# Preparing q and k of the next pair of heads during the second head of the pair before, in the attention of a two-layer decoder

## The chip, the core and the metric

The kernel runs on one core of a Trainium2 chip. A core has five engines that run side by side, each with its own queue that is worked off strictly in order: PE (TensorE, matrix multiplications and transposes), DVE (VectorE), ACT (ScalarE), POOL (GpSimd) and SP (SyncE, which here only issues transfers). PE's weight loads are shown as PEld; they overlap its multiplications. The metric is the time of one execution on the device in microseconds (us), lower is better.

## The reference

The program is a decoder of two layers over 512 tokens of 1024 features, in float32. Each layer is attention, a projection with a residual, and an MLP with a squared ReLU. Layer 0 mixes 8 heads of dilated attention (kind "a") with 8 heads of sliding-window attention that share two key heads (kind "b"); layer 1 has 16 heads of forgetting attention (kind "c"). A head has 64 features; q and k are normalised per head.

```python
def reference(x, ...):
    for layer in range(DEPTH):
        h = rms_norm(x, g_mix[layer])
        if layer % 2 == 0:
            x = x + even_mixer(h, ...)     # heads a and b
        else:
            x = x + odd_mixer(h, ...)      # heads c
        h = rms_norm(x, g_mlp[layer])
        x = x + squared_relu_mlp(h, w_up[layer], w_down[layer])
    return x

def forgetting_attention(q, k, v, log_f):          # one block of 128 queries
    s = jnp.einsum("bqhd,bshd->bhqs", qb, k) * scale
    s = s + jnp.transpose(cq, (0, 2, 1))[..., None] - c_k[:, :, None, :]
    s = jnp.where((key_pos[None, :] <= t[:, None])[None, None], s, -jnp.inf)
    p = jax.nn.softmax(s, axis=-1)
    return jnp.einsum("bhqs,bshd->bqhd", p, v)
```

## The kernel before

Float32 products are made of three products of a high and a low part, so that every weight tile is split first (`whi` on POOL or ACT, `wlo` on POOL or DVE) and every projection is three matmuls: `pj` in the input projections (lines 231 to 233) and `op` in the output projection (lines 164, 167, 168).

Heads are worked in pairs, because two heads of 64 features fill the 128 partitions. `get(p_)` prepares pair p_: `head_T` (line 263) transposes 128 columns of the normalised q, and for the kinds a and c of k, into a PSUM bank named `qkT`, four transposes each. `prep_q` turns it into the tile `Q` with, for each head, a copy on ACT (line 277) and a subtraction on DVE (line 278). `prep_k` makes a tile `K` for each head (ACT line 159, DVE line 160), then SP copies half of it to the other partitions with a transfer (line 290). For the kind b, K is made once before the first pair, and `get` prepares q alone afterwards.

Then come the two heads of the pair (`scores`, line 302). For each of four query blocks PE makes the scores `S` (lines 325, 326, for kind c a mask at 328), DVE adds a bias and takes the minimum (`P`, `negm`, line 339), ACT takes the exponential (line 342), DVE the reciprocal (line 345), and POOL or ACT scales the row. `values` (line 353) transposes P on PE (`PT`, line 362), splits it on ACT and DVE (lines 374, 375), and multiplies by V (`O`, line 382); ACT and DVE add the two halves into `yf` (lines 385, 386). The values of a head are made while the scores of the following head are, one step behind.

For the kind c each head's bias is a transfer of its own (line 311). The buffers that matter: `qkT`, `S`, `PT` and `O` all take one of four PSUM banks (tag `pB`); there are two Q tiles, three K tiles, and two bias tiles.

All of this is one generator, `attend`. `run` advances it against a second generator of dense work, mostly input projections of a later group, by counting steps. A scheduler then orders the instructions within each engine, starting from that program order and moving some of them past each other; it also picks the free bank. There are seven groups: a(0), b and a(1) in layer 0, c(0) to c(3) in layer 1; a group of kind a or c has two pairs and b has four.

Of the kernel before, what the change touches and what calls it, by code (L numbers as in the profile page):

```python
# [37 lines left out]
NORM = 'vgvg'  # L38
PSC = 'ggga'
GRAIN = 4  # L40
STARTPIN = 4
JPIN = 1
PEPIN = True
# [29 lines left out]
def trunk(ctx, tc, x, g_mix, g_mlp, w_in_even, a_q_gain, a_k_gain, b_q_gain, b_k_gain, b_sinks,  # L73
# [46 lines left out]

    cnt = {"hi": 0, "start": STARTPIN}

# [69 lines left out]
    def layer_attention(li, hT, w_in, w_out, stats=None):  # L192


        with ExitStack() as c2:
# [11 lines left out]
            def project(cols, use, pat=PAT_ATT, ahead=False):  # L207
# [6 lines left out]
                for k0 in range(0, DC, kw):  # L214
# [9 lines left out]
                    for m in range(NT if last else kw):  # L224
                        for k, t in ([(k0 + kk, m) for kk in range(kw)] if last else [(k0 + m, t) for t in range(NT)]):
# [8 lines left out]
                            pairs += 1  # L234
                            if pairs % GRAIN == 0:
                                yield GRAIN / 32 * n
                use(outs)
# [153 lines left out]
            def head_values(prev):  # L391
                if prev is None:
                    return
                pr, kind, V, vs, yf, j, n = prev
                yield from values(pr, kind, V, vs, yf, j)
                if j:
                    y = slot(f"y{li}_{n}")
                    ys[n] = y
                    split(y[:, 0], y[:, 1], yf, "act", YLO)

            last_head = [None]

            def attend(get, koff, V, vslot, kind, h0, np_, y0):

                for p_ in range(np_):
                    q, kk = get(p_)
                    yf = ap.tile([P, 512], F32, tag="yf", bufs=1, name="yf")
                    yield
                    for j in range(2):
                        h = h0 + 2 * p_ + j  # L410
                        pr = []
                        old = head_values(last_head[0])
                        for i, _ in enumerate(scores(q, kk[j], j, kind, h, pr)):
                            yield
                            if i >= LAGS["abc".index(kind)] and next(old, 0) is None:
                                yield
                        for _ in old:
                            yield
                        last_head[0] = (pr, kind, V(), vslot(2 * p_ + j), yf, j, y0 + p_)
# [89 lines left out]
            if li == 0:  # L509
# [7 lines left out]
                def att_a(g):  # L517
                    def get(p_):
                        qk = st["qk", g]
                        return prep_q(qk, p_ * P), prep_k(qk, 256 + p_ * P, gg[:, 0:1])  # L520
                    return attend(get, 256, lambda: st["v", g], lambda j: j, "a", 4 * g, 2, 2 * g)
# [7 lines left out]
                def att_b():  # L529
                    def get(p_):  # L530
                        if p_ == 0:
                            st["kb"] = prep_k(st["k", "b"], 0, gg[:, 1:2])
                        k = st["kb"][p_ // 2]
                        return prep_q(st["qk", "b"], p_ * P), [k, k]
                    return attend(get, 0, lambda: st["v", 3], lambda j: j // 4, "b", 0, 4, 4)

                tables, first, qk0 = make_tables(ap, dist, lt, lb), start(ap, hT), qk_a(0)
                next(tables)
                for i, n in enumerate((1, 1 + 8 // GRAIN, 1 + 8 // GRAIN, 1 + 8 // GRAIN)):
                    cnt["start"] = i < STARTPIN  # L540
                    next(first)
# [4 lines left out]
                cnt["start"] = False  # L546
                for _ in range(8 // GRAIN):
                    next(qk0)
# [8 lines left out]
            else:  # L557
# [12 lines left out]
                def att_c(g):  # L570
                    def get(p_):
                        qk = st["qk", g]
                        return prep_q(qk, p_ * P), prep_k(qk, 256 + p_ * P, gg[:, 2:3])
                    return attend(get, 256, lambda: st["v", g], lambda j: j, "c", 4 * g, 2, 2 * g)
# [166 lines left out]
    def mlp(li, accs, attention_end, last):  # L741
# [5 lines left out]
        with ExitStack() as c2:  # L747
# [468 lines left out]
            return hn, lambda: col_stats(token_sums(res["ssum2"]))  # L1216

    accs, end = layer_attention(0, [], w_in_even[0], w_out_even[0])
    hT, stats = mlp(0, accs, end, False)
    accs, end = layer_attention(1, hT, w_in_odd[0], w_out_odd[0], stats)  # L1220
    mlp(1, accs, end, True)

# [21 lines left out]
```

## Time and profile before

| what | value |
|---|---|
| runs of the kernel | 1172.76 us median of 3 (1170.35 to 1174.13) |
| the profiled execution, its own time | 1169.99 us |
| its span | 1168.2 us |
| instructions | 17496 |
| PE busy / weight loads busy | 98% / 84% of the span |
| DVE, ACT, POOL busy | 75%, 55%, 17% |
| attention of layer 0, attention of layer 1 (rough limits) | 46 to 222 us, 610 to 825 us |

The span runs from the first instruction to the last; the execution's own time is 1.8 us longer. Busy time is the time in which an engine works on at least one instruction. An engine's idle time is put down to what ended it.

### The profile page before, as it was taken

The page shows a single profiled execution, that of the slowest core. Times are in us where ns is not written, and L with a number is a line of the kernel's source. Part 1 is how long each engine was busy: PE and PEld are TensorE (multiplying, and loading weights), DVE is VectorE, ACT ScalarE, POOL GpSimd, SP SyncE. Part 2 cuts the span into 40 slices and gives each one's busy share as a digit, 9 for nine tenths or more (in the row PEclk, how much of TensorE's full clock was granted, in tenths as well). Part 3 has the DMA queues.
Part 4 walks back from the last instruction along what each step waited for, and adds up shares of the span by engine and source line. Part 5 has one row for each costly group of instructions (what it writes and reads, how often), then busy time and mean ns, then how long its engine had stood idle before and what let it go on. Part 6 is the DMA issues. An engine that isn't in the chain of part 4 may idle for free.

```text
span 1168.2 us, 17496 instructions
## 1 busy us (share of the span) xinstructions
PE 1146.4 (98%) x6256; PEld 981.4 (84%) x6256; DVE 879.8 (75%) x1870; ACT 646.6 (55%) x1349; POOL 203.0 (17%) x296
## 2 busy tenths in 40 slices
PE   8999989999999999999999999999999999999998
PEld 7987878887988988988887888888888888888887
DVE  7878999969947847855647877788858749669676
ACT  6556867655445545444335685656756455465452
POOL 1445434200000000000155445332100000000000
PEclk9999999999999999999999999999999999999999
DMA  7532024132332332333443323343430721623403
GB/s 257 160 91 73 19 73 145 58 123 73 101 117 91 91 108 91 96 121 108 148 127 109 103 89 110 100 124 112 163 106 3 232 91 51 202 73 108 148 34 109
DMA packets 100655, 126.57 MB, mean 108 GB/s; under 512 B 6184, under 2 KB 79944, under 8 KB 100568
## 3 DMA queue, kind: packets, MB, share of 16 engines
q1 hardware_dynamic: 99384, 121.23, 34.0%
q10 hardware_dynamic: 608, 2.13, 0.5%
q0 software_dynamic: 576, 2.10, 0.4%
q8 instruction: 49, 0.80, 0.3%
q14 instruction: 38, 0.31, 0.1%
HBM read 112.29 MB, written 6.32 MB: 102 GB/s over the span
## 4 chain that ended last, share of the span: by engine, by line
PE 82%; DVE 9%; DMA 3%; ACT 2%; POOL 1%; issue 1%; SPq 0%; ACTq 0%; POOLq 0%; DVEq 0%
PE up L164 10%; PE up L167 10%; PE up L168 10%; PE pj L231 4%; PE pj L233 4%; PE pj L232 4%; PE O L382 3%; PE PT L362 2%; PE Y L1023 2%; PE Y L1022 2%; PE Y L1020 2%; PE op L168 2%; PE op L164 2%; PE op L167 2%; PE S L325 2%; DVE wlo L155 1%
## 5 line engine op out<-in xcount | busy, mean ns | idle before, releaser
L164 PE MATMUL up<-xin,whi 128*128 128x512 f32 x512 | 200.5, 392 | 0.0
L168 PE MATMUL up<-xin,whi 128*128 128x512 f32 x512 | 199.3, 389 | 0.0
L167 PE MATMUL up<-xin,wlo 128*128 128x512 f32 x512 | 199.2, 389 | 0.0
L769 ACT CAST whi<-wraw 128x512 fp32r<-128x512 f32 x228 | 139.2, 619 | 105.5 <-PE up L168 47.3
L770 DVE TENSOR_TENSOR wlo<-wraw,whi 128x512 fp32r<-128x512 f32 x228 | 151.7, 686 | 53.7 <-ACT whi L769 53.5
L168 PEld LDWEIGHTS up<-xin,whi 128*128 128x128 f32 x512 | 96.1, 188 | 20.1
L164 PEld LDWEIGHTS up<-xin,whi 128*128 128x128 f32 x512 | 96.1, 188 | 19.9 <-issue 0.2
L167 PEld LDWEIGHTS up<-xin,wlo 128*128 128x128 f32 x512 | 96.2, 188 | 19.7 <-issue 0.2
L342 ACT ACTIVATE P<-P,negm 128x128 f32<-128x128 f32 (+5 forms) x128 | 69.6, 544 | 51.8 <-DVE negm L339 47.9
L231 PE MATMUL pj<-whi,hn 128*128 128x512 f32 (+2 forms) x256 | 88.7, 346 | 0.0
L951 ACT ACTIVATE u<-up 128x512 f32<-128x512 f32 x64 | 38.3, 598 | 90.9 <-PE up L168 90.9
L233 PE MATMUL pj<-whi,hn 128*128 128x512 f32 (+2 forms) x256 | 86.9, 339 | 0.0
L232 PE MATMUL pj<-wlo,hn 128*128 128x512 f32 (+2 forms) x256 | 86.8, 339 | 0.0
L152 POOL TENSOR_SCALAR whi<-wraw 128x512 fp32r<-128x512 f32 x88 | 61.1, 696 | 141.5 <-PE pj L233 121.3
L790 DVE TENSOR_TENSOR t<-u 128x256 f32<-128x256 f32 x56 | 23.2, 424 | 63.3 <-ACT u L1094 61.5
L155 POOL TENSOR_TENSOR wlo<-wraw,whi 128x512 fp32r<-128x512 f32 x48 | 64.4, 1345 | 20.8 <-ACT whi L150 18.1
L231 PE MATMUL pj<-whi,h 128*128 128x512 f32 (+1 forms) x192 | 65.6, 348 | 0.7 <-DVE v L160 0.7
L232 PE MATMUL pj<-wlo,h 128*128 128x512 f32 (+1 forms) x192 | 65.3, 341 | 0.2 <-DVE wlo L155 0.2
L233 PE MATMUL pj<-whi,h 128*128 128x512 f32 (+1 forms) x192 | 65.5, 343 | 0.0
L350 POOL TENSOR_SCALAR P<-P,rden 128x256 f32<-128x256 f32 (+2 forms) x96 | 47.7, 500 | 90.8 <-DVE rden L345 90.1
L155 DVE TENSOR_TENSOR wlo<-wraw,whi 128x512 fp32r<-128x512 f32 (+1 forms) x72 | 49.7, 697 | 17.5 <-POOL whi L152 9.8
L374 ACT CAST PT<-PT 128x256 fp32r<-128x256 f32 (+3 forms) x128 | 49.5, 405 | 19.3 <-PE PT L362 18.5
(229 smaller groups left out, 3051.7 us busy)
## 6 DMA issues: line engine op xcount, KB each, us to landing
wraw<-in_w_up SPq DMA_DIRECT2D x64, 512.0 KB, 4.0
wraw<-in_w_down SPq DMA_DIRECT2D x56, 512.0 KB, 4.2
wraw<-in_w_in_odd SPq DMA_DIRECT2D x36, 256.0 KB, 3.4
mraw<-in_w_down SPq DMA_DIRECT2D x16, 512.0 KB, 4.7
K<-K SPq DMA_DIRECT2D x26, 256.0 KB
wraw<-in_w_in_even SPq DMA_DIRECT2D x10, 512.0 KB, 4.0
wraw<-in_w_in_even SPq DMA_DIRECT2D x16, 256.0 KB, 4.5
xl<-xsp SPq DMA_DIRECT2D x8, 512.0 KB
```

The source lines that it names most:

```text
L152: nc.gpsimd.tensor_scalar(dst_h, src, 1.0, 1.0, op0=OP.mult, op1=OP.mult)
L155: in_order((nc.gpsimd if lo == "pool" else nc.vector).tensor_sub(dst_l, src, dst_h.bitcast(F32)))
L164: m = nc.tensor.matmul(o, wh, xh, start=start, stop=False, skip_group_check=more)
L167: nc.tensor.matmul(o, wl, xh, start=False, stop=False, skip_group_check=more)
L168: nc.tensor.matmul(o, wh, xl, start=False, stop=stop, skip_group_check=more)
L231: nc.tensor.matmul(o, xh, hi[:, :n], start=k == 0, stop=False)
L232: nc.tensor.matmul(o, xh, lo[:, :n], start=False, stop=False)
L233: nc.tensor.matmul(o, xl, hi[:, :n], start=False, stop=k == DC - 1)
L342: nc.scalar.activation(p[:, :ne], p[:, :ne], AF.Exp, scale=-1.0, bias=negm[:, i:i + 1], accum_out=den[:, i:i + 1])
L374: nc.scalar.copy(dst[:, 0], pt[:, :n])
L769: sca(nc.scalar.copy(dst_h, src))
L770: late.append(lambda: vec(nc.vector.tensor_sub(dst_l, src, dst_h.bitcast(F32))))
```

## The change

`attend` gets a list `pair`. When the second head of a pair (j = 1) has had its first query block of scores recorded (i = 0, the constant PRE), and there is a next pair in the group, `get(p_ + 1)` is called there and its result is kept; the next pair takes it from the list. Nothing else is changed: no instruction is added or removed. The first pair of each of the seven groups is prepared where it was; one pair is moved in each of the six groups of kind a and c (q and k), and three in b (q alone).

```diff
@@ -400,10 +401,12 @@
             last_head = [None]
 
+            pair = []
+
             def attend(get, koff, V, vslot, kind, h0, np_, y0):
 
                 for p_ in range(np_):
-                    q, kk = get(p_)
+                    q, kk = pair.pop(0) if pair else get(p_)
                     yf = ap.tile([P, 512], F32, tag="yf", bufs=1, name="yf")
                     yield
                     for j in range(2):
@@ -412,6 +415,8 @@
                         old = head_values(last_head[0])
                         for i, _ in enumerate(scores(q, kk[j], j, kind, h, pr)):
                             yield
+                            if j and i == PRE and p_ + 1 < np_:
+                                pair.append(get(p_ + 1))
                             if i >= LAGS["abc".index(kind)] and next(old, 0) is None:
                                 yield
```

How the instructions stand now. In the rows below, lines of the changed kernel are one higher than before in these functions (267 becomes 268, and so on).

PE in group c(1), before, from the last values of the first head of pair 0 to the first scores of pair 1. `pj` is the dense work, of which 24 rows stand between the transposes and the scores.

```order
L382 MATMUL O<-PT,v_6422 128x512 x2
L382 MATMUL O<-PT,v_6422 128x384 x2
L382 MATMUL O<-PT_6423,v_6422 128x256
L267 MATMUL qkT<-ident,qk 128x128
L382 MATMUL O<-PT_6423,v_6422 128x256 x3
L267 MATMUL qkT<-ident,qk 128x128 x7
L233 MATMUL pj_7563<-whi,hn 128x512
...
L232 MATMUL pj_7563<-wlo,hn 128x512
L325 MATMUL S<-K,Q 128x256
```

The same engine and group in the changed kernel: first the second head of pair 0, into which the transposes are put, then the place where pair 1 begins.

```order
L268 MATMUL qkT<-ident,qk 128x128 x8
L326 MATMUL S<-K,Q 128x256
L327 MATMUL S<-K,Q 128x256
L329 LDWEIGHTS identb
L329 MATMUL S<-maskb,identb 128x128
L363 MATMUL PT<-ident,P 128x128 x4
L234 MATMUL pj_7560<-whi,hn 128x512
L326 MATMUL S<-K,Q 128x384
...
L383 MATMUL O<-PT_6423,v_6422 128x256
L326 MATMUL S<-K,Q 128x256
L383 MATMUL O<-PT_6423,v_6422 128x256 x3
```

The transposes have moved up by about one head, the 24 dense matmuls that followed them are spread over that head and the next, and pair 1 begins among the values of the head before it. After the scores of 384 columns come 11 `pj` and then the next three transposes `PT`, which in the built program take the bank that q's `qkT` leaves.

DVE at the same place, before, where the four conversions of Q and K follow each other:

```order
L386 TENSOR_TENSOR yf<-O,yf 64x512
L278 TENSOR_TENSOR Q<-qkT,Q 64x512
L160 SCALAR_TENSOR_TENSOR K<-qkT,gg,K 64x512
L278 TENSOR_TENSOR Q<-qkT,Q 64x512
L160 SCALAR_TENSOR_TENSOR K<-qkT,gg,K 64x512
L155 TENSOR_TENSOR wlo<-wraw,whi 128x512
L339 ISA P,negm<-S,bias 128x128
```

And in the changed kernel:

```order
L387 TENSOR_TENSOR yf<-O,yf 64x512
L340 ISA P,negm<-S,bias 128x256
L340 ISA negm 128x1
L346 RECIPROCAL rden<-den 128x1
L156 TENSOR_TENSOR y_1_7543<-yf,y_1_7543 128x512
L279 TENSOR_TENSOR Q<-qkT,Q 64x512
L161 SCALAR_TENSOR_TENSOR K<-qkT,gg,K 64x512
L346 RECIPROCAL rden<-den 128x1
L279 TENSOR_TENSOR Q<-qkT,Q 64x512
L376 TENSOR_TENSOR PT<-PT 128x512
L161 SCALAR_TENSOR_TENSOR K<-qkT,gg,K 64x512
L340 ISA P,negm<-S,bias 128x384
```

The conversions now stand between the softmax steps of the second head, and one step of it (the 384 columns) stands behind the last of them.

SP in group c(0), before: the two transfers of K for pair 1 stand behind two weight loads and the second bias load.

```order
L183 DMA wraw<-in_w_in_odd 128x2x256 x2
L311 DMA bias<-csp 128x512
L183 DMA wraw<-in_w_in_odd 128x4x256
L311 DMA bias<-csp 128x512
L183 DMA wraw<-in_w_in_odd 128x4x256
L290 DMA K<-K 64x1024 x2
```

And in the changed kernel, where they have moved ahead of those three:

```order
L184 DMA wraw<-in_w_in_odd 128x2x256 x2
L312 DMA bias<-csp 128x512
L291 DMA K<-K 64x1024 x2
L184 DMA wraw<-in_w_in_odd 128x4x256
L312 DMA bias<-csp 128x512
L184 DMA wraw<-in_w_in_odd 128x4x256
```

## Rows read from the trace of the kernel before

**Rows 1.** The page: busy us, share of the span and instructions of each engine.
```profile
PE 1146.4 (98%) x6256; PEld 981.4 (84%) x6256; DVE 879.8 (75%) x1870; ACT 646.6 (55%) x1349; POOL 203.0 (17%) x296
```

**Rows 2.** Windows: stretch, its us, busy us by engine, PE's clock, DMA, GB/s.
```profile
46.00:107.00 61.00, 58.11 (x339) 49.70 (x338) 47.29 (x135) 32.97 (x84) 31.24 (x44) 1.00 0.33 96
107.00:180.00 73.00, 69.45 (x451) 60.26 (x450) 68.10 (x216) 54.88 (x160) 33.28 (x72) 1.00 0.16 46
180.00:222.00 42.00, 41.00 (x210) 33.18 (x209) 37.97 (x86) 25.77 (x60) 15.60 (x20) 1.00 0.41 126
610.00:700.00 90.00, 87.79 (x529) 74.03 (x528) 70.14 (x196) 56.82 (x139) 43.03 (x57) 1.00 0.36 103
700.00:825.00 125.00, 124.10 (x757) 106.71 (x756) 98.52 (x255) 74.02 (x175) 49.83 (x64) 1.00 0.38 112
```

**Rows 3.** PE's waits over the span: us in total, times, longest us.
```profile
PE S L325 <- DMA K<-K: 2.6, 3, 1.2
PE S L325 <- DVE Q L278: 1.8, 2, 1.5
PE S L325 <- DVE yf L386: 1.8, 2, 1.6
```

**Rows 4.** Timeline of PE: start us, us, instruction, [idle before <- what ended it].
```profile
151.84 0.39 PE L325 MATMUL S<-K,Q 128*128 128x256 f32 x1 [1.52 <-DVE Q L278]
...
161.52 0.39 PE L325 MATMUL S<-K,Q 128*128 128x256 f32 x1 [1.61 <-DVE yf L386]
...
649.66 0.36 PE L325 MATMUL S<-K,Q 128*128 128x256 f32 x1 [0.88 <-DMA K<-K]
...
795.56 0.36 PE L325 MATMUL S<-K,Q 128*128 128x256 f32 x1 [0.47 <-DMA K<-K]
```

**Rows 5.** Timeline of PE where pair 1 of a(0) is prepared.
```profile
71.34 1.03 PE L267 MATMUL qkT<-ident,qk 128*128 128x128 f32 x8
72.14 0.47 PE L231 MATMUL pj<-whi,h 128*128 128x512 f32 x1
72.45 0.40 PE L232 MATMUL pj<-wlo,h 128*128 128x512 f32 x1
...
77.47 0.28 PE L325 MATMUL S<-K,Q 128*128 128x256 f32 x1
```

**Rows 6.** Timeline of ACT there.
```profile
71.98 0.58 ACT L277 CAST Q<-qkT 64x512 fp32r<-64x512 f32 x1 [2.59 <-PE qkT L267]
...
73.31 0.58 ACT L277 CAST Q<-qkT 64x512 fp32r<-64x512 f32 x1 [0.17 <-DVE Q L278]
```

**Rows 7.** Timeline of DVE there.
```profile
72.59 0.68 DVE L278 TENSOR_TENSOR Q<-qkT,Q 64x512 fp32r<-64x512 f32 x1 [0.23 <-ACT Q L277]
73.31 0.74 DVE L160 SCALAR_TENSOR_TENSOR K<-qkT,gg,K 64x512 fp32r<-64x512 f32 x1
74.08 0.70 DVE L278 TENSOR_TENSOR Q<-qkT,Q 64x512 fp32r<-64x512 f32 x1
74.81 0.76 DVE L160 SCALAR_TENSOR_TENSOR K<-qkT,gg,K 64x512 fp32r<-64x512 f32 x1
```

**Rows 8.** The chain that ended last, at pair 1 of c(0): start us, us, what.
```profile
646.05 3.47 DMA K<-K
```

**Rows 9.** Windows: the stretch of group b with the long waits.
```profile
147.00:163.00 16.00, 12.77 (x97) 11.60 (x96) 15.78 (x45) 10.01 (x31) 8.26 (x13) 1.00 0.19 66
```

**Rows 10.** Timeline of DVE in that stretch.
```profile
147.85 1.52 DVE L308 SCALAR_TENSOR_TENSOR bias<-dist,lb 128x256 f32<-128x256 f16 x1
149.37 0.41 DVE L308 SCALAR_TENSOR_TENSOR bias<-dist,lb 128x256 f32<-128x256 f16 x1
...
157.67 3.00 DVE L260 TENSOR_TENSOR qk<-qk,rs 128x512 f32<-128x512 f32 x2
```

**Rows 11.** Timeline of PE in c(0): scores and transposes of one head.
```profile
657.28 0.36 PE L325 MATMUL S<-K,Q 128*128 128x256 f32 x1
...
657.67 0.61 PE L362 MATMUL PT<-ident,P 128*128 128x128 f32 x4
658.03 0.42 PE L325 MATMUL S<-K,Q 128*128 128x384 f32 x1
...
658.58 0.55 PE L362 MATMUL PT<-ident,P 128*128 128x128 f32 x3
```

More of the change, by code (lines that the diff above doesn't have):

```diff
@@ L40 @@
 GRAIN = 4
+PRE = 0
 STARTPIN = 4
```

## The prediction

> **What bounds the kernel now.** I read the page first: PE is busy for 1146.4 us of the span of 1168.2 [rows 1], so it stands still for 21.8 us in all, and no reordering can give back more than that. The change touches attention alone, so the second view is the windows of the attention stretches [rows 2]: they last 391 us, PE is busy in 380.45 of them (58.11 + 69.45 + 41.00 + 87.79 + 124.10), and 10.55 us are left. PE's clock column is 1.00 throughout. DVE is the second engine: 68.10 of 73 us in the stretch that holds group b, but only 98.52 of 125 in the last one. Third come PE's waits [rows 3]. Three of them are for the transfer of K (2.6 us), two for the subtraction of Q (1.8 us), two for `yf` (1.8 us). Fourth, the timeline tells which of these belong to a pair that the change moves [rows 4]: 1.52 us before the first scores of the last pair of b, 0.88 us at pair 1 of c(0), 0.47 us at pair 1 of c(3). That is 2.87 us at three of the nine moved places; at the other six PE does not wait at the pair's first scores. The rest of the waits for K and Q (the longest for K, 1.2 us, among them) belong to first pairs of a group, which stay, and the 1.61 us for `yf` stand inside a head.
>
> **What is moved.** Nothing is added, so the whole sum is waits that go and waits that come. A pair of kind a or c moves eight transposes, four conversions on ACT, four on DVE and two transfers on SP; a pair of b moves four transposes and two conversions on each engine. Why the old place costs so little is seen at pair 1 of a(0) [rows 5]: the transposes start at 71.34 and the first scores at 77.47, and the 6.1 us between are filled with 23 dense matmuls, one every 0.228 us (72.45 to 77.47 is 22 of them). The preparation is long, but PE is not idle in it. In the new order this dense work is still there and stands elsewhere, so hiding the preparation better is worth nothing where it is already hidden.
>
> **What is gained.** At c(0) about 12 us of PE work now lie between the transposes and pair 1, counted from the new order at the rates of [rows 5, 11], and a K transfer took 3.47 us [rows 8]: the 0.88 us go. At c(3) it is about 10 us; the 0.47 us go. The 1.52 us in b are another matter. DVE is busy 15.78 of 16 us there, and PE 12.77 [rows 9]. What makes Q late is that DVE is behind: one bias operation takes 1.52 us where the next of the same shape takes 0.41, and two scalings of `qk` for a later group take 3.00 us together [rows 10]. None of this is moved. Q's two subtractions (0.7 us each) leave the critical place, but the same DVE work must be done in the same stretch, and an engine with 0.22 us to spare in 16 gives back nothing but what is taken out of it. PE will meet DVE's lag at another scores or transposes. The bounds for this stretch are 0 (the lag only moves) and 3.13 us (both long waits of [rows 4] go, 1.52 + 1.61); I take about half of it, 1.5, since pair 3 starts with Q ready and the two subtractions no longer stand between DVE's backlog and PE. Gain: 0.88 + 0.47 + 1.5 = 2.85 us.
>
> **What is lost.** The conversions now stand inside a head, where the four `pB` banks turn over fastest, and two banks (one in b) are held until the conversions are done. Undisturbed they run in turn: ACT copies Q at 71.98, DVE subtracts at 72.59, ACT copies the second half at 73.31, DVE ends it at 74.78, and K ends at 75.57 [rows 6, 7]. Counted from the first transpose at 71.34, q's bank is free after 3.44 us and k's after 4.23. In c(1), the changed order gives PE this work before it needs q's bank: transposes 0.80 us (71.34 to 72.14), scores 0.39, four transposes 0.36, one dense matmul 0.23, scores of 384 columns 0.55 [rows 11], eleven dense matmuls 2.51; together 4.84 us. But ahead of Q's conversions stand the copy of `yf`, its addition on DVE, the copy of y on ACT and Q's own copy, each 0.6 to 0.7 us by the shapes of [rows 6, 7], so about 2.5 us; then Q, K, a reciprocal and Q on DVE, 2.3 us; with some 0.1 us at each of four or five changes of engine this is about 5.2 us, and PE waits 0.4. c(2) has the same order: 0.8 us for both. For a(0), a(1), c(0) and c(3) the same count of PE's work comes to 4.2 to 5.1 us against 3.44 undisturbed, and I take 0.1 each. In b the bank is needed again only after 5 us and Q alone is quick: 0. Bounds per place with q and k: 0, and 1.5 us if two more softmax steps stand ahead of each conversion; for six places 0 to 9 us. Loss taken: 0.8 + 0.4 = 1.2 us.
>
> On SP, K's transfers now pass weight loads and one bias load in c(0), and in c(2) and c(3) similar ones. They cost something only if SP waits at them while a load behind them is due. In c(1) the bias of the next head is still issued ahead of them, and the weight loads are for matmuls many microseconds away: 0, with an upper bound of one K transfer, 3.47 us, if K is late in one group.
>
> **The sum.** 1.2 lost less 2.85 gained is 1.65 us less: the profiled execution's 1169.99 us would become 1168.3. The median of the runs shown is 1172.76, 2.8 above that execution, and I apply the same difference to it: 1171.1 us. About 0.3% (3.5 us) is what a measurement of this kernel can tell from no change, and the sum is half of it.
>
> **Rivals.**
> *The lag only moves* (no gain in b, the losses as taken): 0.88 + 0.47 against 1.2 is nothing, 1172.6 us. For it speaks DVE at 15.78 of 16 us; against it, that Q is no longer behind that backlog.
> *The attention runs ahead.* With no preparation between pairs, the softmax chain of the next pair starts at once and the later waits shrink too: all long waits of [rows 4] (4.48 us), plus part of the remaining 6 us of idle time in [rows 2]; 4 to 7 us less, 1166 to 1169. It decides if DVE still has work it can pull forward. [...] The dense rows 0.228 us apart [rows 5] show a filled stream, and what a reordering can return is idle time, so I leave the chance of this rival at 0.2.
> *Banks run short* (the other side). With two of four banks held, PE waits inside the second head: if the conversions come 1.1 us or more later than PE needs them at each of the six places with q and k, the loss is over 6.4 us, exceeds the gain by 3.5, and the kernel is slower; at the bound of 9 us it comes to 1179. For it: four conversions in turn, DVE order with `y` ahead of them. Against it: dense work has been placed in between. [...]
> *Nothing happens* is not open: the order shows the moves in all nine places.
>
> **Chances.** Forecast (0.5 to 3.4 us less) 0.45; the lag only moves 0.16; the attention runs ahead 0.20; banks short, beyond 3.5 us, 0.19. The first two are within 0.3%, with 0.02 of the forecast's edge going to faster. So faster 0.22, same 0.59, slower 0.19. The likeliest case alone gives 1169 to 1172.5; the range takes in most of both outer cases: 1166.5 to 1177.5.
>
> **What would show it.** Right: the waits for K at pair 1 of c(0) and c(3) gone from PE's list, the transposes `qkT` directly followed by scores, windows of layer 1 shorter by about 1 us, and PE's idle time in the stretch of b down from 3.2 to about 1.7 us. Lost terms right: waits of 0.3 to 0.6 us at `PT` in c(1) and c(2), ended by the subtraction of Q. Wrong: new waits of PE above 1 us ended by DVE Q or K, or by `negm`, inside second heads; or stretches of b where PE idles less than 1 us.

## The result, and the profile after

The changed kernel takes 1175.68 us (median of 20 executions) against 1172.23 us of 20 of the kernel before: a ratio of 1.0032, 95% interval 1.0025 to 1.0038. It is slower by about 3.7 us, where 1.65 us less had been forecast. The profiled execution has a span of 1172.9 us (before 1168.2). First the page's busy row, which answers to [rows 1]:

```profile
PE 1149.4 (98%) x6256; PEld 982.5 (84%) x6256; DVE 879.2 (75%) x1870; ACT 648.3 (55%) x1349; POOL 201.6 (17%) x296
```

The instruction counts are the same. PE is busy for 3.0 us more and idle for 1.7 us more in these two executions. To see where, I cut the span at marks of PE: from the first transpose `qkT` to the first matmul `up` of MLP 0 (attention of layer 0), from there to the first matmul `pc` of layer 1 (mostly MLP 0), and from there to the last `op` (attention of layer 1). Windows of the kernel before (columns as in [rows 2]):

```profile
46.98:227.79 180.81, 173.37 (x1014) 146.93 (x1012) 158.52 (x443) 117.47 (x308) 79.14 (x132) 1.00 0.28 82
227.79:578.34 350.55, 347.46 (x2019) 308.07 (x2018) 248.83 (x453) 177.75 (x322) 1.47 (x3) 1.00 0.34 103
578.34:830.83 252.49, 249.38 (x1482) 213.18 (x1480) 190.37 (x495) 144.12 (x335) 111.77 (x141) 1.00 0.40 117
```

And of the changed kernel:

```profile
47.63:231.46 183.83, 173.88 (x1014) 146.22 (x1012) 157.78 (x443) 118.13 (x308) 77.97 (x132) 1.00 0.27 81
231.46:582.84 351.38, 348.50 (x2020) 309.47 (x2018) 248.91 (x453) 177.71 (x322) 1.48 (x3) 1.00 0.34 103
582.84:835.47 252.63, 250.50 (x1482) 213.18 (x1480) 190.33 (x495) 144.87 (x335) 111.62 (x141) 1.00 0.40 117
```

Attention of layer 0 is 3.02 us longer, and PE's idle time in it went from 7.44 to 9.95 us. Layer 1 is even (+0.14), but not for lack of an effect: its idle time fell from 3.11 to 2.13 us, and its busy time rose by 1.12 us with the same 1482 instructions. MLP 0, which the change does not touch, is 0.83 us longer; that is the clock (last section). The remaining 0.65 us lies before the first `qkT`; over sixteen traces, all with the same work there, that mark stands anywhere from 46.98 to 49.34 us.

PE's waits of the changed kernel, total us, times, longest us, answer to [rows 3]:

```profile
PE op L168 <- DVE wlo L156: 2.5, 1, 2.5
...
PE S L326 <- DMA K<-K: 1.5, 2, 1.1
...
PE S L326 <- DVE yf L387: 1.2, 1, 1.2
PE O L383 <- ACT PT L375: 1.1, 2, 0.9
...
PE S L326 <- DVE Q L279: 0.7, 2, 0.4
```

The waits for K fell from three to two, those for Q from 1.8 to 0.7 us and for `yf` from 1.8 to 1.2. But the first row is new. The timeline of PE around it, in answer to the first two of [rows 4]:

```profile
159.84 0.39 PE L326 MATMUL S<-K,Q 128*128 128x256 f32 x1 [1.20 <-DVE yf L387]
169.77 0.50 PE L168 MATMUL op<-y,wlo 128*128 128x512 f32 x1 [2.52 <-DVE wlo L156]
```

The 1.52 us are gone and 1.61 became 1.20. Then the output projection, the dense work of a(1), stands still for 2.52 us because a low part of its first weight tile is late. DVE's timeline says why:

```profile
165.31 0.69 DVE L279 TENSOR_TENSOR Q<-qkT,Q 64x512 fp32r<-64x512 f32 x1 [0.33 <-ACT Q L278]
166.03 0.74 DVE L161 SCALAR_TENSOR_TENSOR K<-qkT,gg,K 64x512 fp32r<-64x512 f32 x1
166.81 0.69 DVE L279 TENSOR_TENSOR Q<-qkT,Q 64x512 fp32r<-64x512 f32 x1
167.51 0.69 DVE L307 SCALAR_TENSOR_TENSOR bias<-dist,lt 128x512 f32<-128x512 f16 x1
168.24 0.76 DVE L161 SCALAR_TENSOR_TENSOR K<-qkT,gg,K 64x512 fp32r<-64x512 f32 x1
169.02 0.69 DVE L156 TENSOR_TENSOR wlo<-wraw,whi 128x512 fp32r<-128x512 f32 x1
```

`wlo` stands behind the whole preparation of pair 0 of a(1), a pair that the change does not move, and behind it in turn PE's `op`. In the kernel before, DVE made the same `wlo` 19 us earlier, inside b and ahead of the late Q there:

```profile
149.79 0.68 DVE L155 TENSOR_TENSOR wlo<-wraw,whi 128x512 fp32r<-128x512 f32 x1
```

So it is the place in DVE's queue that makes `wlo` late. In the changed kernel its input `whi` was ready from 144.83 us on (POOL), and DVE had no backlog ahead of these rows: it stood idle for 0.33 us before the first of them. The order of the built program shows what the scheduler did: before, 36 `op` matmuls stood ahead of a(1)'s first scores on PE, and now 20. With b's preparation hidden, the attention moved up against the dense work, and pair 0 of a(1) passed the split of the weights.

### The profile page after: what moved, and what is told of

Same layout as the page of the kernel before. It is cut to its first block, busy times and chain, and to the rows that moved or that the text cites. A ratio compares the mean times of both kernels' runs of the same rounds, so it can differ in the third digit from the quotient of the medians.

```text
span 1172.9 us, 17481 instructions
## 1 busy us (share of the span) xinstructions
PE 1149.4 (98%) x6256; PEld 982.5 (84%) x6256; DVE 879.2 (75%) x1870; ACT 648.3 (55%) x1349; POOL 201.6 (17%) x296
## 3 DMA queue, kind: packets, MB, share of 16 engines
q10 hardware_dynamic: 608, 2.13, 0.5%
## 4 chain that ended last, share of the span: by engine, by line
PE 78%; DVE 3%; ACT 2%; issue 1%; POOL 1%; DMA 0%; POOLq 0%; DVEq 0%
PE up L165 10%; PE up L169 10%; PE up L168 10%; PE pj L232 3%; PE pj L234 3%; PE pj L233 3%; PE op L169 2%; PE op L168 2%; PE op L165 2%; PE O L383 2%; PE Y L1025 2%; PE Y L1027 2%; PE Y L1028 2%; PE PT L363 2%; PE Y L1074 1%; PE Y L1077 1%
```

## The experiments

Theory A: the loss is made in layer 0, where DVE's lag in b is no longer met by b's scores but by the output projection's first weight split; layer 1 is about even. Rival B: every early preparation takes a PSUM bank from the scores, and the loss spreads over the nine moved pairs. Rival C: it is the granted clock. DVE's lag is the backlog of [rows 9, 10]: what DVE is asked for arrives late because it is still busy with earlier work. Each ratio below is to the kernel before on the same chip, with its 95% interval; a difference of 0.001 in the ratio is 1.2 us.

**Which moves cost.** A set of groups decides where the preparation is moved; all else is the changed kernel.

```diff
-                            if j and i == PRE and p_ + 1 < np_:
+                            if j and i == PRE and p_ + 1 < np_ and f"{kind}{y0}" in MOVED:
```

Layer 1 alone: 

> Only the four moves of layer 1 (pair 1 of c(0) to c(3)); layer 0 as before. Theory A (the loss is made in layer 0: b's lag on DVE meets the split of the first output weight tile in a(1)): ratio 1.000, within 0.1%, since in layer 1 the 1.0 us of removed waits went into 1.1 us of finer pieces on TensorE. Rival B (an early qkT takes a PSUM bank from the scores at every moved pair, 9 in all, so the 3.5 us spread evenly): 4 of 9, 1.6 us, ratio 1.0013. Rival C (the loss is the granted clock's dip in MLP 0, which comes with any of the orders): ratio 1.002 with a mean clock of 0.997 in most runs.

Measured 1.0012 (1.0003 to 1.0021), 1.4 us over; the mean clock was 0.997 in 6 of 11 executions and 0.998 or higher in the others.

Layer 0 alone: 

> Only the five moves of layer 0 (pair 1 of a(0), pairs 1 to 3 of b, pair 1 of a(1)); layer 1 as before. Theory A: all of the loss, ratio 1.003 (3 to 4 us over before), the wait of op for wlo of 2 to 2.5 us in the trace. Rival B: 5 of 9, 1.9 us, ratio 1.0016. Rival C: ratio 1.002 with the clock's dip.

Measured 1.0034 (1.0022 to 1.0047), from six executions; the wait of `op` for `wlo` is there, 2.53 us.

Group b alone: 

> Only the three moves inside b. Theory A: b's moves alone make the attention stand ahead of the output projection when a(1) begins, so the 2.5 us wait of op for wlo is there and the ratio is 1.002 to 1.003. Rival B: 3 of 9, 1.2 us, ratio 1.001. Rival C: ratio 1.002 with the clock's dip.

Measured 1.0015 (1.0005 to 1.0024), less than A expected and with rival B's 1.001 inside the interval; the wait of `op` for `wlo` is there, 2.53 us.

a(0) and a(1) alone: 

> Only pair 1 of a(0) and of a(1); b and layer 1 as before. Theory A: the waits of 1.52 and 1.61 us in b stay as before and no wait of op for wlo comes; what is left is the new waits inside a(1) (O for PT, 0.9 us over before) and in a(0) (0.6 us): ratio 1.001. Rival B: 2 of 9, 0.8 us, ratio 1.0007. Rival C: ratio 1.002 with the clock's dip.

Measured 1.0009 (1.0000 to 1.0018). The waits in b stay (1.52 and 1.62 us), and there is no wait of `op` for `wlo`.

Layer 0 has most of it, as A said, and rival B's 1.0016 for layer 0 is outside the interval. But B's figures for the other three parts are inside theirs; what tells most against an even loss at every move are the versions further down, where three and four moved pairs make the kernel faster. A was wrong on layer 1, which costs about 1 us (1.4 here, 0.2 and 0.8 for its two halves below). The parts do not add up to the whole: b and a apart make 1.0024, together 1.0034; layers 0 and 1 apart make 1.0046, together 1.0032. Intervals of this width leave room for both differences. The 2.5 us wait comes with b's moves.

**Is it the weight split?** The first output weight tile of layer 0 is loaded and split one step earlier in the program, before a(1) begins; shown is the part of the line that changes. In the kernel before, this edit leaves the order of every engine as it was when the program is built, so no gain by itself is to be expected; it was not run there.

```diff
-chain(out_part([0, 1, 4, 5], True),
+chain(out_part([0, 1, 4, 5], True, None, {0: out_weights([0, 1, 4, 5], 0)}),
```

> All nine moves, and the first output weight tile of layer 0 is prepared one step earlier in the program, so that its wlo stands ahead of a(1)'s first conversions on DVE instead of behind them. Theory A (b's lag costs time because it now meets that split): the 2.5 us wait of op for wlo goes and little takes its place; ratio 1.001 (2 to 2.5 us under the changed kernel). Rival D (DVE's lag is the bound and any order of it costs the same): a wait of about 2 us comes at a(1)'s first scores, for Q or K, and the ratio stays at 1.003.

Measured 1.0005 (0.9995 to 1.0015), 1172.12 us. DVE's timeline in that kernel:

```profile
165.08 0.67 DVE L156 TENSOR_TENSOR wlo<-wraw,whi 128x512 fp32r<-128x512 f32 x1
165.79 0.68 DVE L279 TENSOR_TENSOR Q<-qkT,Q 64x512 fp32r<-64x512 f32 x1
```

and PE's waits of more than 0.45 us between 145 and 190 us:

```profile
160.00 0.39 PE L326 MATMUL S<-K,Q 128*128 128x256 f32 x1 [1.21 <-DVE yf L387]
175.74 0.36 PE L326 MATMUL S<-K,Q 128*128 128x256 f32 x1 [0.70 <-DMA K<-K]
180.63 0.63 PE L363 MATMUL PT<-ident,P 128*128 128x128 f32 x4 [1.11 <-DVE yf L387]
```

`wlo` is ahead of pair 0's preparation, its wait is gone, and some 3 us of the loss with it by the timings (2.05 us by the window of layer 0 in the one trace, 181.78 against 183.83). The edit also brings the scheduler to put 33 `op` matmuls ahead of a(1)'s first scores instead of 20, so it undoes the run-ahead, not the place of one instruction alone. Of the 2.52 us 1.81 came back in a(1) (0.70 and 1.11 us), as rival D has it in part; other waits there shrank.

**The parts of layer 1.** 

> Only pair 1 of c(0) and of c(3), the two places where TensorE waited for K (0.88 and 0.47 us). Theory A (each moved pair of layer 1 costs about 0.3 us in finer pieces of TensorE's stream, whether or not something was waited for): 1.35 less against 0.6 more, ratio 0.9994. Rival E (the removed wait comes back elsewhere in the same group): ratio 1.0005.

Measured 1.0002 (0.9994 to 1.0011), which holds both figures.

> Only pair 1 of c(1) and of c(2), where TensorE waited for nothing before. Theory A: 0.6 to 0.8 us more, made of finer pieces and waits of 0.1 to 0.2 us, ratio 1.0006. As the prediction had it: 0.4 us of wait at PT in each, ratio 1.0007. If the moves cost nothing by themselves: ratio 1.000.

Measured 1.0007 (0.9998 to 1.0015). Neither interval excludes 1, so here the traces have to speak. In the window of layer 1, this is c(1) and c(2) moved, and then a kernel with no pair of layer 1 moved (b alone):

```profile
578.72:831.40 252.68, 249.94 (x1482) 213.11 (x1480) 190.79 (x495) 144.22 (x335) 111.08 (x141) 1.00 0.40 117
```

```profile
582.54:834.18 251.64, 249.31 (x1481) 213.16 (x1480) 190.48 (x495) 144.03 (x335) 112.03 (x141) 1.00 0.40 118
```

PE's busy time in this stretch is 249.28 to 249.38 us in every trace without a move in layer 1, 249.83 to 249.96 with two pairs moved and 250.46 to 250.50 with all four: 0.3 us a pair. What is rising is the number of places where PE goes from one kind of work to another (217 in the order without moves, 223 with c(0) and c(3), 225 with c(1) and c(2), 231 with all). That the one makes the other is argued from these counts alone; it was not tried by itself.

**Versions put together.** 

> The moves of b, c(0) and c(3), with the first output weight tile prepared earlier as in the run before; a(0), a(1), c(1) and c(2) as before the change. Theory A: b's 1.5 us and most of 1.6 us are gained, wlo is no longer waited for, and 0.7 us come from layer 1: ratio 0.998. Rival D: nothing is gained in b, ratio 0.9995 to 1.001.

Measured 0.9980 (0.9971 to 0.9988), 1169.92 us.

> The moves of b alone, with the first output weight tile prepared earlier. Theory A: all of the gain of the run with b, c(0) and c(3) was made in layer 0, about 2 us, and layer 1 gives back what it cost: ratio 0.998 to 0.9985. If c(0) and c(3) had a part of 0.8 us in it, as first expected: ratio 0.9990.

Measured 0.9980 (0.9971 to 0.9988), 1169.64 us. So the gain is layer 0's, and c(0) and c(3) add nothing. Its window of layer 0 and PE's one wait above 0.45 us between 145 and 225 us:

```profile
47.95:226.43 178.48, 173.11 (x1014) 146.43 (x1012) 155.73 (x443) 117.11 (x308) 78.62 (x132) 1.00 0.28 83
```

```profile
159.81 0.39 PE L326 MATMUL S<-K,Q 128*128 128x256 f32 x1 [1.22 <-DVE yf L387]
```

PE idles 5.37 us there against 7.44 before. The version above has the same order in layer 0, and its trace shows less of it: a window of 179.83 us, 6.6 us of idle time, and a wait of 1.10 us for `wlo` at a(1)'s first scores. By the timings of both, b's moves do give back what the prediction hoped for, if the output projection's weights are out of the way.

> All five moves of layer 0, with the first output weight tile prepared earlier; layer 1 as before. Theory A: the moves in a(0) and a(1) together with b's cost 1 to 1.5 us (waits of O for PT and of PT for yf inside a(1)), so the ratio is 0.9995 to 1.000. If a(0) and a(1) cost nothing and layer 1 took the rest: ratio 0.998.

Measured 1.0002 (0.9991 to 1.0013): with a(0) and a(1) moved too, the gain is lost. Which of the two it is:

> The moves of b and of a(1), first output weight tile prepared earlier; a(0) and layer 1 as before. If a(1)'s move takes the 2 us back (its conversions stand ahead of the softmax steps that the output projection's end waits for): ratio 1.000, with waits of O for PT (0.7 us) and of PT for yf (about 1 us) near 180 and 198 us. If a(0)'s does: ratio 0.998.

Measured 1.0006 (0.9996 to 1.0015).

> The moves of b and of a(0), first output weight tile prepared earlier; a(1) and layer 1 as before. If a(1)'s move takes the 2 us back: ratio 0.998, as with b alone. If a(0)'s does: ratio 1.000.

Measured 0.9976 (0.9967 to 0.9984), 1170.08 us beside 1172.55: it beats both kernels, and with the two versions above it is the best found. So it is a(1)'s move. PE's waits of more than 0.45 us in the kernel with b and a(1), between 165 and 185 us:

```profile
170.46 0.35 PE L326 MATMUL S<-K,Q 128*128 128x256 f32 x1 [0.52 <-DMA K<-K]
180.01 0.63 PE L363 MATMUL PT<-ident,P 128*128 128x128 f32 x4 [1.95 <-DVE yf L387]
```

DVE ahead of the second one, and POOL:

```profile
175.69 1.77 DVE L156 TENSOR_TENSOR wlo<-wraw,whi 128x512 fp32r<-128x512 f32 x1
177.39 1.76 DVE L307 SCALAR_TENSOR_TENSOR bias<-dist,lt 128x512 f32<-128x512 f16 x1
179.18 0.68 DVE L387 TENSOR_TENSOR yf<-O,yf 64x512 f32<-64x512 f32 x1
...
180.09 0.69 DVE L279 TENSOR_TENSOR Q<-qkT,Q 64x512 fp32r<-64x512 f32 x1
```

```profile
175.63 2.98 POOL L156 TENSOR_TENSOR wlo<-wraw,whi 128x512 fp32r<-128x512 f32 x2
```

`yf` is late because two DVE instructions that take 0.68 us elsewhere take 1.77 and 1.76 while POOL makes its own two `wlo`; PE needs `yf` to get a bank for `PT`. The other two traces with a(1) moved and the weights earlier have the same: `bias` takes 1.78 and 1.77 us there while POOL makes two `wlo`, and PE waits 1.11 and 0.85 us at `PT` for `yf`. In the kernels without a(1)'s move the waits in this stretch are smaller or others: none above 0.45 us with b alone, 1.01 (for `wlo`) and 0.63 us (for `yf`) with b and a(0). That `bias` meets POOL's `wlo` because a(1)'s preparation has moved is argued from these traces and was not tried by itself.

**Without DVE's lag.** The bias of b is computed once and kept, so the per-head slopes of b are left out. Two lines of the edit; it also gives the kept bias a tile of its own.

```diff
-                elif kind == "b":
+                elif kind == "b" and not one:
+                    st["bb"] = bias
```

> The order of before the change (no pair moved), and in b the bias is computed once instead of for each of the eight heads; this leaves the per-head slopes of b out and takes seven operations of 0.4 to 1.5 us from DVE. If DVE's lag sets the two long waits of b (1.52 and 1.61 us): they shrink to under half, ratio 0.998. If the length of the preparation between pairs sets them: they stay, ratio 1.000.

Measured 0.9972 (0.9963 to 0.9982). The same program again, for its trace:

> The same program as the one with one bias for all heads of b (per-head slopes left out) and no pair moved, for its trace and a second timing. DVE's lag as the cause: the waits of 1.52 us for Q and of 1.61 us for yf in b both under 0.5 us; ratio 0.9972 again.

Measured 0.9971 (0.9960 to 0.9982). PE's waits above 0.45 us between 145 and 225 us are two:

```profile
150.97 0.38 PE L326 MATMUL S<-K,Q 128*128 128x256 f32 x1 [0.58 <-DVE Q L278]
161.79 0.44 PE L363 MATMUL PT<-ident,P 128*128 128x128 f32 x2 [1.13 <-DVE PT L376]
```

The 1.52 us fell to 0.58, the 1.61 us to 1.13 at another place. DVE's load sets most of the waits of b, and seven small operations less on it are worth 3 us. The limit of 0.5 us that was expected is not met, and the scheduler's order is not quite that of before (30 `op` matmuls ahead of a(1)'s first scores, not 36).

> All nine moves, and b's bias computed once (the per-head slopes of b are left out). Theory A: with less lag on DVE the wait of op for wlo shrinks from 2.5 to about 1.5 us, since it still stands behind Q, K and Q of a(1); ratio 1.0005 to 1.001, 3 us over the same kernel without moves. Rival D (DVE is the bound and the order is not): as much as the same kernel without moves, within 1 us.

Measured 1.0013 (1.0004 to 1.0022), 4.5 us over the same kernel without moves. A had expected 1.5 us to be left of the wait of `op` for `wlo` and 3 us of loss. The wait is down to 0.10 us, and still the change costs at least what it did: in the traces layer 0 takes 182.01 us against 178.57. Without the lag in b, PE's waits are at `PT` for `yf` in b (1.33 us) and at `O` for `PT` in a(1) (1.15 and 0.54 us). So neither the lag nor the weight split is needed for a loss of this size. The split is the place at which it shows in the changed kernel, and not the whole cause.

> b's moves with the earlier output weight tile, and one bias for all heads of b (per-head slopes left out). If b's gain comes from DVE's lag alone: none is left to gain, 1.000 of the same kernel without moves (ratio 0.997 to the kernel before). If moving the preparation gains by itself: 2 us less than that, ratio 0.9955.

Measured 0.9996 (0.9987 to 1.0005): 2.5 us over the same kernel without moves. With the lag gone b's moves gain nothing, as A said, but that they cost 2.5 us was expected by neither. The attention does not run ahead here: 29 `op` matmuls stand ahead of a(1)'s first scores, and 30 in the kernel without moves. What PE waits for in this program is not shown, and the cause stays open.

## Why the prediction was wrong

The range held the time, but only because it took in much of the slower rival. The direction was wrong: a gain of 1.65 us was forecast, 3.5 to 3.7 us were lost.

*Waits for K in layer 1* (0.88 and 0.47 us): both are gone, as said. In the changed kernel PE goes from the dense work into pair 1 of c(0) without a pause, 0.12 us after the instruction before:

```profile
648.18 0.28 PE L234 MATMUL pj<-whi,hn 128*128 128x256 f32 x1
648.30 0.28 PE L326 MATMUL S<-K,Q 128*128 128x256 f32 x1
```

The same at c(3). But the 0.47 us at c(3) were in part luck of the trace that was read: of the ten traces in which this pair is not moved, two have a wait of 0.47 or 0.48 us there and the other eight have 0.14 us or less. The first pairs' waits for K stay, as said.

*The gain in b* (1.5 us) came, and more of it, inside the stretch that the prediction looked at. The window of [rows 9] in the changed kernel:

```profile
147.00:163.00 16.00, 14.78 (x117) 14.04 (x117) 15.63 (x62) 12.50 (x40) 7.73 (x17) 1.00 0.00 2
```

PE idles 1.22 us there where it idled 3.23, with DVE about as full as before. For DVE's lag being met elsewhere the prediction had taken half of the two long waits off; here 2.0 us were gained.

*The loss that b's moves bring* was put at nothing, and this is the step that failed. The prediction counted waits that come at the nine moved places alone. Of the DVE work that makes Q late in b it named biases and scalings, said "None of this is moved", and took it that "the same DVE work must be done in the same stretch". One piece that it did not name did move: the split of the output projection's weights went from 149.79 us, ahead of that Q, to 169.02, behind the preparation of pair 0 of a(1), and PE stood at it from 167.25 to 169.77. From 146 to 182 us the waits went from 3.44 us (1.52, 0.10, 1.61, 0.21) to 4.22 (0.11, 1.20, 2.52, 0.39). With the split put back ahead of that pair, b's moves alone are 2.3 us faster than the kernel before; without that, they are 1.8 us slower. *The lag only moves* was the rival nearest to this; it gave the lag the same price in its new place, and the price rose. That a lag of DVE was carried there is not shown: DVE had been idle just before, and the loss is there without the lag too.

*The losses in layer 0* were put at 0.1 us each for a(0) and a(1) and nothing for b. a(0) is about even: a new wait of 0.69 us for `sq` on ACT, and 0.58 us at `O` gone. In b a wait of 0.56 us of scores for `PT` is new, at 119.44 us, in the head that now holds the bank of pair 1's transposes. In a(1) two waits at `O` for `PT` came to 1.41 us, where two of 0.50 us together had stood at `PT`. With the 0.8 us above and half a microsecond of busy time, that makes nearly all of the 3.0 us of layer 0. For a(1) 0.1 us was far too little where b is moved too: with the weights prepared first, adding a(1) to b's moves takes the ratio from 0.9980 to 1.0006, some 3 us.

*The losses in layer 1* (0.4 us each at `PT` in c(1) and c(2), 0.1 at c(0) and c(3), 1.0 in all): the size was about right and the form was not. The 0.4 us were worked out with some 0.1 us for each change of engine, an estimate that the rows do not show: in [rows 6, 7] DVE starts 0.03 us after ACT's copy has ended, and ACT 0.04 us after DVE's subtraction. No new wait of PE above 0.15 us stands in the second heads of c(1) and c(2). What came is 1.12 us more of busy time, 0.3 us at each of the four moved pairs, which the prediction had counted as nothing: it counted waits only. So the windows of layer 1 did not get shorter by the 1 us that was named as a sign of being right. Against the average of nine traces without a move in layer 1 (252.05 us, from 251.64 to 252.57) the four with all its pairs moved, at 252.61 to 252.68, are 0.6 us longer; so the removed waits were paid for in full.

*The attention runs ahead* was right as a mechanism (it does run ahead) and wrong in its sign. PE's idle time in layer 0's attention, 7.44 us before, 9.95 in the changed kernel and 5.37 in the version with b's moves that is 2 us faster, says where the difference lies. The busy share of weight loads does not: it is 81%, 80% and 82% (146.93, 146.22 and 146.43 us of the windows shown), so it moves with the result only because the window does.

*Banks run short* named the right side and the wrong place: its waits of over 1 us for Q, K or `negm` in second heads are not there.

*What stays open.* One trace carries some 1.5 us of scatter in layer 0: the four traces with the order of before in layer 0 have windows of 180.81, 181.02, 181.04 and 182.26 us there, and the two with all five moves 183.83 and 183.77. By the averages the loss in layer 0 is nearer 2.5 than 3.0 us, and its split into single waits is that of one execution; the timings, over many, are what the parts rest on. Why the change costs 4.5 us and b's moves 2.5 us once the lag is gone isn't settled either.

## What to carry to other kernels

A wait hidden in one place can come back at a place that the change does not touch: look in the new order of the busy engine for critical dense work (here the split of the first weights) that ends up behind the attention on the same queue. Where a scheduler reacts to the program order, an early step in one place shifts the balance of the two streams in the next; count what stands ahead of the next group's first scores on both sides. Moves that helped (b, with the weights prepared first) and moves that cost (a(1), and the four of layer 1 together) came in one edit of a few lines, and only trying them apart showed that a version 2 to 3 us faster than before was near. And a wait read from one trace, like the 0.47 us at c(3), may not be there in the next.

## What the runs showed of the hardware

The same DVE instruction of 128x512 took 0.68 us or 1.77 us: `wlo` at 149.79 us in the kernel before, and at 175.69 us in the kernel with b and a(1). `bias` took 0.69 us at 167.51 us in the changed kernel, and 1.76 us in the kernel with b and a(1). There the two stood beside POOL's `wlo`: POOL began at 175.63, DVE's `wlo` was booked from 175.69 to 177.46, and `bias` then lasted to 179.15, just past the end of POOL's two instructions at 178.61. What slows them is not shown; the traces show only that they were slow while POOL worked on its `wlo`.

The granted clock. After a wait of 2.37 or 2.38 us in MLP 0 that every trace has, the clock fell in ten of sixteen profiles and in six it didn't. PE in the changed kernel, start and length of matmuls of 256 columns behind that wait:

```profile
295.17 0.58 PE L1074 MATMUL Y<-t,whi 128*128 128x256 f32 x1 [2.38 <-DVE acc L1090]
295.55 0.42 PE L1077 MATMUL Y<-t,wlo 128*128 128x256 f32 x1
295.76 0.41 PE L1078 MATMUL Y<-t,whi 128*128 128x256 f32 x1
```

The same place before:

```profile
291.50 0.39 PE L1069 MATMUL Y<-t,whi 128*128 128x256 f32 x1 [2.38 <-DVE acc L1085]
291.72 0.28 PE L1072 MATMUL Y<-t,wlo 128*128 128x256 f32 x1
291.83 0.29 PE L1073 MATMUL Y<-t,whi 128*128 128x256 f32 x1
```

They follow each other at 0.21 us instead of 0.11. The clock's column in the changed kernel is 0.50 from 296 to 298 us and 1.00 from 299 us on, and for 290 to 310 us it is 0.91 against 1.00. MLP 0's window is 351.3 to 351.5 us in the ten traces and 350.5 to 350.6 in the six, so it costs about 0.85 us. The same fall followed two of the new waits in layer 0. With b's moves alone the clock's column is 0.57 from 170 to 174 us, right behind the wait of 2.53 us for `wlo`; with b and a(1) it is 0.57 from 181 to 185 us, behind the wait of 1.95 us for `yf`. Over the whole of layer 0's window it is 0.99 in both, and 1.00 with b alone and the weights prepared first. In the changed kernel's own trace the 2.52 us were not followed by one: the column is 1.00 from 170 to 174 us.

The changed kernel's mean clock was 0.997 or lower in 17 of 20 executions, that of the kernel before in 3 of 29, 8 of 35, 14 of 33 and 10 of 30 in the four sets of runs beside the experiments. The means of these are 0.9970 against 0.9980 to 0.9986. One fall takes about 0.0015 from the mean clock (1.000 in the trace before, which has none, 0.997 in the changed kernel's, which has two, with a column of 0.57 from 8 to 12 us and from 295 to 299 us in MLP 0), so at 0.85 us a fall some 0.6 to 0.9 us of the loss goes with the clock: an estimate. The later arrival at that wait does not decide it: the clock fell in traces that came out of it at 291.4 and 292.5 us, and not in ones at 293.4 and 294.6. Rival C, that the clock is the whole of it, is out: layer 0 is longer by 3.0 us at a clock of 1.00, and by as much in the trace of layer 0's moves alone.
